# Two heads alternate in halves of TensorE, and the PSUM banks are shared out anew

## The chip, the cores and the metric

The kernel runs on one core of a Trainium2 chip. A core has the engines PE (TensorE, matrix products), DVE (VectorE), ACT (ScalarE), POOL (GpSimd) and SP (SyncE, which here issues most DMAs), each with an instruction order of its own that it works through without overtaking; semaphores tie the orders together. PSUM, the memory that PE writes to, has eight banks of 512 fp32 values on each of 128 partitions. The metric is the device time of one execution in microseconds, the median of several.

PE's array of 128 rows by 128 columns can be used as two halves: two of 64 rows (the operands lie on partitions 0 to 63 or 64 to 127) or two of 64 columns (the result lies on the one or the other 64 partitions). Views of the profile write the used part ahead of a product's shape: `128*128` is the full array, `64*128` one half of the rows, `128*64` one half of the columns.

## The reference

The reference is a model of two blocks on 256 tokens of 1024 channels. The first block has two layers, each a mixer and a mixture of 16 experts; the second has four mixers.

```python
# first block, layer 0: gated linear attention beside dense attention (latent and context)
# first block, layer 1: attention in a window, 16 heads on 2 of keys and values, with a context and a sink
s = einsum('bqhgd,bkhd->bhgqk', q, k) * Dh ** -0.5
p = softmax(concatenate([where(mask, s, -inf), sink]))[..., :-1]
o = einsum('bhgqk,bkhd->bqhgd', p, v)
# second block: h = h + rms_norm(mixer(rms_norm(h))) four times, all causal, with linear biases
# 1 nsa: compressed, selected and window attention of 16 heads on 4, gated
p_s = masked_softmax(q @ ksel - slopes * dist, dist >= 0);  o_s = p_s @ vsel      # the same for the window
# 2 diff: p = masked_softmax(...) of two maps;  a = p[0] - lam * p[1];  o = a @ v
# 3 dilated: three groups of keys, merged by their log-sum-exp
o = sum(softmax(stack(lses)) * stack(outs))
# 4 stick: a = exp(log_sigmoid(logits) + between), between = reversed sums of log_sigmoid(-logits)
```

Every mixer ends with a gate silu(z) or the like and an output projection.

## The kernel before, in words

The kernel keeps all tokens on the chip and streams the weights (285 MB) past them. Large products are made exact enough by splitting both operands into a high and a low part of type float32r: `gemm` (L239) issues three products for each 128 channels, L243, L244 and L245, usually 256 columns wide. Scores are split the same way: `scores` (L414) issues L416, L417 and L418 for one head, whose 64 channels lie on one half of the partitions, so these products use half of the rows. Values are multiplied as plain fp32, which the profile records as two matmuls each; two heads use one half of the columns each (L915 in nsa, L1094 in `attend`, L719 and L720 in stick).

A head's way in nsa, diff and dilated: scores into a bank of PSUM; DVE adds the bias and takes the maximum (L891 in nsa); ACT takes the exponential and its sum (L893); PE turns the weights, three transposes into one bank (`turn_causal`, L438); ACT copies the bank to SBUF (L440); PE multiplies by the values. `attend` does the same for the even and the odd layer with `turn` (L1131: transposes L1141, copies L1143). In stick, a head's sums over later keys take products of their own (L710 to L712) between two passes of ACT.

The eight banks carry tags, taken from one pool for the whole kernel: two `mm` for projections, three `s` for scores, two `t` for turned weights and small products, one `o` for outputs. A tile of a tag waits until the oldest tile of the tag has been read.

In odd, `queries(0)` projects the first queries into an `mm` bank, `norm_rope` (L1044: square L1049, a product with ones L1051, root L267 and L268, times L1054) normalises them, then come the keys in the same way, the values, and the four rounds of four heads each, every round with the next round's queries ahead of its scores. The weights of the experts that follow are issued by SP behind those of odd's output projection.

A scheduler orders the instructions of each engine when the kernel is built; the order stays as it is on the chip. It takes the instructions in program order where it can and fills with others where its plan has an engine wait. nsa has 8 rounds of two heads with two branches each: 16 branches of two heads. Beside them stand the products of the gate and of the queries. Stick has 8 pairs of heads, diff 8 heads of two maps, dilated 4 heads of three groups.

Of the kernel before, what the change touches and what calls it, by code (L numbers as in the profile page):

```python
# [10 lines left out]
F32 = mybir.dt.float32  # L11
# [3 lines left out]
AF = mybir.ActivationFunctionType  # L15
# [28 lines left out]
def constants():  # L44
    """Arrays that depend on shapes alone: groups of them side by side in [128, n] arrays."""
# [36 lines left out]
    # GLA: sums over tokens up to / from t, over the gate's 16; which token pairs a level holds  # L82
# [14 lines left out]
    # rotary tables by channel of a pair of heads  # L97
# [10 lines left out]
class K:  # L108
    def __init__(self, ctx, tc, A, groups):
# [5 lines left out]
        self.ps = ctx.enter_context(tc.tile_pool(name="ps", bufs=1, space=PSUM))  # L115
# [34 lines left out]
    def psum(self, tag, bufs):  # L150
        return self.ps.tile([128, 512], F32, name="ps_" + tag, tag=tag, bufs=bufs)

    def mm(self):
        return self.psum("mm", 2)

    def pss(self):
        return self.psum("s", 3)

    def pst(self):
        return self.psum("t", 2)  # L160

    def pso(self):
        return self.psum("o", 1)
# [25 lines left out]
    def wload(self, src, kt=KT, pool=None, eng=None):  # L189
        """src: DRAM [kt*128, n] -> raw tile view [128, kt, n]."""  # L190
# [14 lines left out]
    def wload_parts(self, src, kt):  # L205
        """The same in the room of a split weight's parts; gives a list of [128, n]."""
# [32 lines left out]
    def gemm(self, out, sh, sl, mh, ml, ks=range(KT)):  # L239
        """out[M, N] = sum_k stat[k]^T mov[k], both given as hi, lo lists of [128, .]."""  # L240
# [6 lines left out]
    def gemm_cm(self, out, w, m, x):  # L247
        """channel-major: out[128 channels, tokens]"""
# [4 lines left out]
    def gemm_tm(self, out, w, t, x, cols=slice(None)):  # L253
        """token-major: out[128 tokens, columns]"""
# [1986 lines left out]
```

## Time and profile before

| | us |
|---|---|
| median of 3 runs | 1591.15 (1583.63 to 1591.83) |
| profiled execution: its span | 1586.3 |
| median less the span | 4.85 |

The profiled execution's time beyond its span is not among the runs; the span is what all views divide up. Its stages, from the first to the last instruction of each by PE's timeline:

| stage | from, to (us) |
|---|---|
| even layer | 0 to 387 |
| its experts | 387 to 629 |
| odd layer | 629 to 738 attention, to 764 output projection |
| its experts (latent alone) | 764 to 921.5 |
| nsa | 921.5 to 985 keys, values and first scores; to 1089 the rounds; to 1129 output projection |
| diff | 1129 to 1280 |
| dilated | 1280 to 1417 |
| stick | 1417 to 1586.3, its pairs from 1455 to 1557 |

Matmuls overlap in their pipeline, so PE's busy time runs from the first start to the last end of a row of products without a gap; how long one product holds the array is read from the distance between starts. Some records of matmuls can be missing from a trace.

### The profile page before, as it was taken

The page shows a single profiled execution, that of the slowest core. Times are in us where ns is not written, and L with a number is a line of the kernel's source. Part 1 is how long each engine was busy: PE and PEld are TensorE (multiplying, and loading weights), DVE is VectorE, ACT ScalarE, POOL GpSimd, SP SyncE. Part 2 cuts the span into 40 slices and gives each one's busy share as a digit, 9 for nine tenths or more (in the row PEclk, how much of TensorE's full clock was granted, in tenths as well). Part 3 has the DMA queues.
Part 4 walks back from the last instruction along what each step waited for, and adds up shares of the span by engine and source line. Part 5 has one row for each costly group of instructions (what it writes and reads, how often), then busy time and mean ns, then how long its engine had stood idle before and what let it go on. Part 6 is the DMA issues. An engine that isn't in the chain of part 4 may idle for free.

```text
span 1586.3 us, 26615 instructions
## 1 busy us (share of the span) xinstructions
PE 1467.7 (93%) x10361; PEld 1173.3 (74%) x10361; DVE 977.2 (62%) x2043; ACT 810.3 (51%) x1644; POOL 321.5 (20%) x311
## 2 busy tenths in 40 slices
PE   5999987989599898999799999999999999989998
PEld 3766765666477676766566688777899889889888
DVE  4654669853577556875412376555777685867665
ACT  3454544543466554664211345565556654746664
POOL 2000124412211103111000031232321241422231
PEclk7999999999799998999899999999999999999999
DMA  8700248964799987214899946121454445345320
GB/s 266 233 27 1 94 159 280 309 226 147 220 327 332 354 271 264 87 58 140 287 315 368 337 141 217 55 81 54 138 162 132 133 148 172 122 143 168 106 82 27
DMA packets 243689, 284.71 MB, mean 179 GB/s; under 512 B 14546, under 2 KB 227554, under 8 KB 243556
## 3 DMA queue, kind: packets, MB, share of 16 engines
q1 hardware_dynamic: 236644, 259.85, 50.6%
q0 software_dynamic: 6912, 23.07, 4.4%
q8 instruction: 85, 1.39, 0.4%
q14 instruction: 48, 0.39, 0.1%
HBM read 275.56 MB, written 9.44 MB: 180 GB/s over the span
## 4 chain that ended last, share of the span: by engine, by line
PE 44%; DVE 4%; ACT 1%; DMA 1%; issue 0%; POOL 0%; another core or an unknown queue 0%; DVEq 0%; POOLq 0%
PE ps_mm L243 6%; PE ps_mm L244 6%; PE ps_mm L245 5%; PE ps_mm L1954 4%; PE ps_mm L332 3%; PE ps_mm L546 2%; PE ps_s L416 2%; PE ps_t L1994 2%; PE ps_o L915 1%; PE ps_t L438 1%; PE ps_s L417 1%; DVE wl L231 1%; PE ps_s L418 1%; DMA w<-exp_w_gate 1%; PE ps_t L1937 1%; PE ps_s L546 1%
## 5 line engine op out<-in xcount | busy, mean ns | idle before, releaser
L231 DVE TENSOR_TENSOR wl<-w,wh 128x1024 fp32r<-128x1024 f32 x257 | 321.4, 1257 | 155.4 <-ACT wh L230 151.9
L230 ACT CAST wh<-w 128x1024 fp32r<-128x1024 f32 x261 | 270.3, 1042 | 139.3 <-PE ps_mm L245 67.6
L243 PE MATMUL ps_mm<-uh,wl 128*128 128x256 f32 x720 | 210.4, 292 | 0.7 <-DVE v L561 0.6
L244 PE MATMUL ps_mm<-ul,wh 128*128 128x256 f32 x720 | 205.6, 286 | 0.0
L245 PE MATMUL ps_mm<-uh,wh 128*128 128x256 f32 x720 | 204.3, 284 | 0.0
L243 PEld LDWEIGHTS ps_mm<-uh,wl 128*128 128x128 f32 x720 | 135.6, 188 | 8.2 <-issue 1.8
L244 PEld LDWEIGHTS ps_mm<-ul,wh 128*128 128x128 f32 x720 | 135.7, 188 | 3.3 <-issue 1.2
L245 PEld LDWEIGHTS ps_mm<-uh,wh 128*128 128x128 f32 x720 | 135.7, 188 | 1.9 <-issue 0.7
L243 PE MATMUL ps_mm<-wh,xl 128*96 128x256 f32 x256 | 76.6, 299 | 3.0 <-DVE xl L409 3.0
L244 PE MATMUL ps_mm<-wl,xt 128*96 128x256 f32 x256 | 75.0, 293 | 0.0
L245 PE MATMUL ps_mm<-wh,xt 128*96 128x256 f32 x256 | 73.9, 289 | 0.0
L1010 PE MATMUL ps_mm<-w,cond 128*32 128x256 f32 x768 | 55.3, 405 | 17.5 <-DMA w<-mod_w 8.7
L2036 PE MATMUL ps_s<-w,ht 128*96 128x512 f32 x128 | 57.6, 593 | 0.0
L1954 PE MATMUL ps_mm<-w,xt 128*64 128x256 f32 x384 | 52.7, 383 | 0.1
L243 PE MATMUL ps_mm<-hh,wl 128*128 128x512 f32 (+2 forms) x136 | 47.9, 353 | 2.5 <-DVE qn L1054 2.5
L1010 PEld LDWEIGHTS ps_mm<-w,cond 128*32 128x32 f32 x768 | 22.0, 113 | 37.8 <-DVE mod L1017 11.4
L295 POOL TENSOR_TENSOR rawsq<-rawsq 128x256 f32<-128x256 f32 x16 | 13.9, 869 | 177.7 <-ACT rawsq L294 177.7
L244 PE MATMUL ps_mm<-hl,wh 128*128 128x512 f32 (+2 forms) x136 | 48.0, 354 | 0.9 <-DVE hl L1035 0.9
L243 PEld LDWEIGHTS ps_mm<-wh,xl 128*96 128x96 f32 x256 | 43.5, 170 | 7.2 <-DVE xl L409 4.0
L245 PE MATMUL ps_mm<-hh,wh 128*128 128x512 f32 (+2 forms) x136 | 46.8, 344 | 0.0
L332 PE MATMUL ps_mm<-ol,wh 128*128 128x256 f32 x144 | 42.4, 295 | 3.6 <-DVE ol L587 3.6
L332 PE MATMUL ps_mm<-oh,wl 128*128 128x256 f32 x144 | 41.9, 295 | 2.9 <-ACT oh L587 1.7
(659 smaller groups left out, 4082.4 us busy)
## 6 DMA issues: line engine op xcount, KB each, us to landing
w<-mod_w SPq DMA_DIRECT2D x48, 1024.0 KB, 7.5
w<-exp_w_up SPq DMA_DIRECT2D x28, 1024.0 KB, 11.2
w<-exp_w_gate SPq DMA_DIRECT2D x27, 1024.0 KB, 13.5
w<-exp_w_down SPq DMA_DIRECT2D x27, 1024.0 KB, 11.7
w<-b_w_in SPq DMA_DIRECT2D x16, 1024.0 KB, 5.5
w<-d_w_in SPq DMA_DIRECT2D x16, 1024.0 KB, 5.5
w<-a_w_in SPq DMA_DIRECT2D x14, 1024.0 KB, 8.1
w<-c_w_in SPq DMA_DIRECT2D x14, 1024.0 KB, 5.0
```

Source lines behind the costliest of these rows:

```text
L230: nc.scalar.copy(hv, raw[:, i:i + c])
L231: (nc.gpsimd if i and pool_too else nc.vector).tensor_sub(lv, raw[:, i:i + c], hv.bitcast(F32))
L243: nc.tensor.matmul(out, sl(k), mh(k), start=k == ks[0], stop=False)
L244: nc.tensor.matmul(out, sh(k), ml(k), start=False, stop=False)
L245: nc.tensor.matmul(out, sh(k), mh(k), start=False, stop=k == ks[-1])
L332: nc.tensor.matmul(p[:, 256 * m:256 * m + 256], w[a][k][:, 128 * m:128 * m + 128], b[:, k], start=k == 0 and m == 0 and j == 0, stop=k == ...
L416: nc.tensor.matmul(out, ql, kh, start=True, stop=False)
L546: nc.tensor.matmul(ps[i][:, 256 * t:256 * t + 256], x[a][:, k, ts], w[b][k], start=k == 0 and t == 0 and j == 0, stop=k == KT - 1 and t == ...
L1010: nc.tensor.matmul(p[j:j + 32, :256], self.cond[:, k], w[:, k], start=k < 4, stop=k >= 4)
L1954: nc.tensor.matmul(p[64 * a:64 * a + 64, 256 * j:256 * j + 256], xt[:, k, off + 64 * a:off + 64 * a + 64], w[j][a][k], start=k == 0, stop= ...
L1994: nc.tensor.matmul(p[64 * a:64 * a + 64, :], ht[:, f, 64 * a:64 * a + 64], w[a][f][:, cs], start=f == 0, stop=f == 1)
L2036: nc.tensor.matmul(p, ht[:, f], w[:, f, cs], start=f == 0, stop=f == 1)
```

## The change

Scores of two heads, one on each half of PE's rows, are now issued in turn, product by product, into the two banks of one tile (`pair`); values of two heads, one on each half of the columns, are issued in turn, and the first of them is made to wait for both heads' turned weights (`behind`). In diff, dilated and one branch of nsa the first 128 queries are multiplied with 128 keys instead of 256. Dilated takes two heads in one pass and merges each behind the three groups of both. The pool of banks is opened anew ahead of odd and ahead of its experts: four banks become two two-bank tiles `s2`, and one `mm` (in odd) or one `t` (from the experts on) is given up for that. Odd's output projection and the experts' sums use the two-bank tiles; other small tiles of the experts take `t` and `o` in turn. Comments were taken out too; lines of the changed kernel are some 20 to 40 further down.

```diff
+    def banks(self, **n):
+        self.pstack.close()
+        self.ps = self.pstack.enter_context(self.tc.tile_pool(name="ps", bufs=1, space=PSUM, reuse_waits="tile"))
+        self.nbanks = n
+        self.either = itertools.cycle((self.pst, self.pso))
...
+    def pair(self):
+        if "s2" not in self.nbanks:
+            return [self.psum("s"), self.psum("s")]
+        t = self.ps.tile([128, 2, 512], F32, name="ps_s", tag="s2", bufs=self.nbanks["s2"])
+        return [t[:, 0], t[:, 1]]
...
+    def behind(self, ins, *others):
+        for o in others:
+            self.tc.add_manual_dep(ins, o.name, mybir.DependencyInfo(mybir.DependencyClass.Sync, mybir.DependencyReason.DATA), reason="side by side")
...
-    def scores(self, out, qh, ql, kh, kl):
-        nc.tensor.matmul(out, ql, kh, start=True, stop=False)
-        nc.tensor.matmul(out, qh, kl, start=False, stop=False)
-        nc.tensor.matmul(out, qh, kh, start=False, stop=True)
+    def scores(self, outs, qs, ks):
+        for j, (a, b) in enumerate(((1, 0), (0, 1), (0, 0))):
+            for out, q, k in zip(outs, qs, ks):
+                self.nc.tensor.matmul(out, q[a], k[b], start=j == 0, stop=j == 2)
+    def scores_causal(self, q, k, mq, mk):
+        pvs = [p.rearrange("p (t n) -> p t n", t=2) for p in self.pair()]
+        rs = (slice(0, 64), slice(64, 128))
+        for t in range(2):
+            ts, n = slice(128 * t, 128 * t + 128), 128 * t + 128
+            self.scores([pv[:, t, :n] for pv in pvs], [[x[r, mq, ts] for x in q] for r in rs], [[x[r, mk, :n] for x in k] for r in rs])
+        return pvs
...
+    def spread(self, po, vs, ats):
+        first = None
+        for kt, (of, n) in enumerate(((0, 256), (256, 128))):
+            for half, (at, _) in enumerate(ats):
+                i = self.nc.tensor.matmul(po[64 * half:64 * half + 64, 256 - n:256], vs[half][kt], at[:, of:of + n],
+                                          start=kt == 0, stop=kt == 1).ins
+                first = first or i
+        self.behind(first, *(i for _, i in ats))
...
 # dilated
-            for hd in range(H):
+            for j in range(H // 2):
+                es, mxs, sms = ([wk.tile([128, G, n], F32, name=name, tag=name, bufs=3) for _ in range(2)]
+                                for name, n in (("e", 384), ("mx", 2), ("sm", 2)))
                 for g in range(G):
+                    pvs = self.scores_causal(q[:2], q[2:], 2 * g + j, 2 * g + j)
...
+                for i, (e, mx, sm) in enumerate(zip(es, mxs, sms)):
+                    self.merge(wk, e, mx, sm, v, 2 * j + i, o)
...
 # stick
-                        nc.tensor.matmul(po[r, :256], v[:, 0, vs], a[:, :256], start=True, stop=False)
-                        nc.tensor.matmul(po[r, 128:256], v[:, 1, vs], a[:, 256:384], start=False, stop=True)
+                    ps = self.pair()
+                    rs = (slice(0, 64), slice(64, 128))
+                    for ks, qs, os in ((slice(0, 128), slice(0, 256), slice(0, 256)), (slice(128, 256), slice(128, 256), slice(256, 384))):
+                        self.scores([p[:, os] for p in ps], [(kh[r, m, ks], kl[r, m, ks]) for r in rs],
+                                    [(qh[r, m, qs], ql[r, m, qs]) for r in rs])
+                    ats = [self.stick_weights(wk, p, suffix, before, minus, diag) for p in ps]
+                    self.spread(po, [[v[:, kt, 64 * (hd + i):64 * (hd + i) + 64] for kt in range(2)] for i in range(2)], ats)
...
 # odd's output projection; the experts of the latent
+            outs = self.pair() + self.pair()
-                p = self.mm()
+            for p, (c, w) in zip(outs, enumerate(ws)):
...
-                acc = [self.pss() for _ in range(3)] + [self.pso()]
+                acc = self.pair() + self.pair()
-                        p = self.pst()
+                        p = next(self.either)()
...
 # nsa, keys of the blocks
-                p = self.mm() if i else self.pss()
+                if i:
+                    p = self.mm()
+                else:
+                    p, ph = self.pair()
...
 # program
+            self.banks(mm=1, s2=2, t=2, o=1)
             self.odd(mods[1][:, 2])
+            self.banks(mm=2, s2=2, t=1, o=1)
             self.moe_lat(1, moe[1], self.x, gsf[1], mods[1][:, 3], mods[1][:, 5], ahead=(
```

The order of PE shows what moved. First a pair of heads in stick, before (L416 to L418 are scores, L243 and L244 the gate's products; 128x256 is the result):

```order
L243 MATMUL ps_mm_15328<-uh_14823,wl_15325 128x256
L416 MATMUL ps_s_15259<-qkh_15076,qkl_15142 128x256
L417 MATMUL ps_s_15259<-qkl_15077,qkh_15141 128x256
L418 MATMUL ps_s_15259<-qkh_15076,qkh_15141 128x256
L416 MATMUL ps_s_15259<-qkh_15076,qkl_15142 128x128
L417 MATMUL ps_s_15259<-qkl_15077,qkh_15141 128x128
L418 MATMUL ps_s_15259<-qkh_15076,qkh_15141 128x128
L416 MATMUL ps_s_15284<-qkh_15076,qkl_15142 128x256
L417 MATMUL ps_s_15284<-qkl_15077,qkh_15141 128x256
L418 MATMUL ps_s_15284<-qkh_15076,qkh_15141 128x256
L416 MATMUL ps_s_15284<-qkh_15076,qkl_15142 128x128
L417 MATMUL ps_s_15284<-qkl_15077,qkh_15141 128x128
L418 MATMUL ps_s_15284<-qkh_15076,qkh_15141 128x128
L244 MATMUL ps_mm_15328<-ul_14824,wh_15324 128x256
```

and after (L438 is the one line of all scores now, L263 the gate's; `x2` are the two heads, one bank each of tile ps_s_15161):

```order
L265 MATMUL ps_mm_15107<-uh_14778,wh_15103 128x256
L438 MATMUL ps_s_15161<-qkh_15030,qkl_15096 128x256 x2
L438 MATMUL ps_s_15161<-qkl_15031,qkh_15095 128x256 x2
L438 MATMUL ps_s_15161<-qkh_15030,qkh_15095 128x256 x2
L438 MATMUL ps_s_15161<-qkh_15030,qkl_15096 128x128 x2
L438 MATMUL ps_s_15161<-qkl_15031,qkh_15095 128x128 x2
L438 MATMUL ps_s_15161<-qkh_15030,qkh_15095 128x128 x2
L263 MATMUL ps_mm_15280<-uh_14778,wl_15273 128x256
```

The twelve products stay together; the heads take turns where one followed the other.

Second, two branches in nsa's rounds, before (L438 are the transposes, L915 the values):

```order
L438 MATMUL ps_t_10059<-k_all_68,e_10045 128x128 x3
L915 MATMUL ps_o_10020<-at_10043,vsw_9170 64x256
L416 MATMUL ps_s_10189<-KH_9275,ql_9953 128x256
L417 MATMUL ps_s_10189<-KL_9276,qh_9952 128x256
L438 MATMUL ps_t_10081<-k_all_68,e_10069 128x128 x3
L418 MATMUL ps_s_10189<-KH_9275,qh_9952 128x256
L416 MATMUL ps_s_10189<-KH_9275,ql_9953 128x256
L417 MATMUL ps_s_10189<-KL_9276,qh_9952 128x256
L418 MATMUL ps_s_10189<-KH_9275,qh_9952 128x256
L244 MATMUL ps_mm_10845<-ul_9145,wh_10836 128x256
L245 MATMUL ps_mm_10845<-uh_9144,wh_10836 128x256
L243 MATMUL ps_mm_10845<-uh_9144,wl_10841 128x256
```

and after, in the eighth to thirteenth branch (L467 are the transposes, L438 scores, L477 values):

```order
L467 MATMUL ps_t_10317<-k_all_68,e_10310 128x128 x3
L467 MATMUL ps_t_10330<-k_all_68,e_10323 128x128 x3
L438 MATMUL ps_s_10457<-KH_9263,ql_10225 128x128 x2
L438 MATMUL ps_s_10457<-KL_9264,qh_10224 128x128 x2
L438 MATMUL ps_s_10457<-KH_9263,qh_10224 128x128 x2
L438 MATMUL ps_s_10457<-KH_9263,ql_10225 128x256 x2
L438 MATMUL ps_s_10457<-KL_9264,qh_10224 128x256 x2
L438 MATMUL ps_s_10457<-KH_9263,qh_10224 128x256 x2
L477 MATMUL ps_o_10292<-at_10321,vsw_9158 64x256
L477 MATMUL ps_o_10292<-at_10334,vsw_9158 64x256
L477 MATMUL ps_o_10292<-at_10321,vsw_9158 64x128
L477 MATMUL ps_o_10292<-at_10334,vsw_9158 64x128
```

Transposes, scores and values come in blocks of two heads, and from the seventh branch's end to the thirteenth's no product of the gate or the queries stands between them; before, such products stand in every round.

Third, the start of odd, before (L245 ends the keys' product, L1051 are the ones-products of queries and keys, L243 begins the next):

```order
L244 MATMUL ps_mm_6409<-hl_6054,wh_6405 128x512
L245 MATMUL ps_mm_6409<-hh_6053,wh_6405 128x512
L1051 MATMUL ps_t_6384<-nsq_6382,k_rope_6301 128x512
L1051 MATMUL ps_t_6436<-nsq_6434,k_rope_6301 128x512
L243 MATMUL ps_mm_6455<-hh_6053,wl_6402 128x512
```

and after (L1086 is the ones-product, here of the keys; that of the queries stands 25 rows ahead of it, before the keys' first product):

```order
L264 MATMUL ps_mm_6413<-hl_6054,wh_6409 128x512
L265 MATMUL ps_mm_6413<-hh_6053,wh_6409 128x512
L1086 MATMUL ps_t_6440<-nsq_6438,k_rope_6305 128x512
L263 MATMUL ps_mm_6459<-hh_6053,wl_6406 128x512
L264 MATMUL ps_mm_6459<-hl_6054,wh_6405 128x512
```

Each ones-product now stands between two projections, where both stood behind both projections.

## Rows read from the trace of the kernel before

**Rows 1.** The page: busy us, share of the span and instructions of each engine.

```profile
PE 1467.7 (93%) x10361; PEld 1173.3 (74%) x10361; DVE 977.2 (62%) x2043; ACT 810.3 (51%) x1644; POOL 321.5 (20%) x311
```

**Rows 2.** Busy time by stretch: us, PE, PEld, DVE, ACT, POOL, clock, DMA share, GB/s.

```profile
629.00:738.00 109.00, 106.59 (x652) 74.86 (x652) 79.62 (x168) 66.22 (x137) 11.33 (x10) 1.00 0.22 70
...
764.00:921.50 157.50, 148.15 (x1075) 93.83 (x1073) 49.23 (x134) 38.30 (x81) 0.06 (x1) 0.97 0.94 317
...
985.00:1089.00 104.00, 103.78 (x709) 79.87 (x707) 57.32 (x223) 63.69 (x185) 32.37 (x31) 1.00 0.21 69
1089.00:1129.00 40.00, 33.65 (x241) 29.79 (x241) 22.61 (x39) 19.06 (x36) 6.04 (x6) 0.96 0.34 106
...
1455.00:1557.00 102.00, 101.81 (x752) 90.85 (x751) 64.36 (x91) 62.58 (x117) 29.87 (x35) 1.00 0.30 94
```

**Rows 3.** PE's timeline in stick: start, us, line, operation, tiles, used array, shape.

```profile
1454.77 0.28 PE L244 MATMUL ps_mm<-ul,wh 128*128 128x256 f32 x1
1454.89 0.27 PE L245 MATMUL ps_mm<-uh,wh 128*128 128x256 f32 x1
1455.09 0.38 PE L416 MATMUL ps_s<-qkh,qkl 64*128 64x256 f32 x1
1455.31 0.28 PE L417 MATMUL ps_s<-qkl,qkh 64*128 64x256 f32 x1
1455.43 0.28 PE L418 MATMUL ps_s<-qkh 64*128 64x256 f32 x1
...
1456.07 0.27 PE L418 MATMUL ps_s<-qkh 64*128 64x128 f32 x1
1456.27 0.39 PE L243 MATMUL ps_mm<-uh,wl 128*128 128x256 f32 x1
```

**Rows 4.** PE's timeline in odd: scores of two heads, then of one.

```profile
705.99 0.51 PE L416 MATMUL ps_s<-KH,ql 64*128 64x512 f32 x2
706.32 0.42 PE L417 MATMUL ps_s<-KL,qh 64*128 64x512 f32 x2
706.55 0.42 PE L418 MATMUL ps_s<-KH,qh 64*128 64x512 f32 x2
706.79 0.39 PE L416 MATMUL ps_s<-KH,ql 64*128 64x512 f32 x1
707.02 0.38 PE L417 MATMUL ps_s<-KL,qh 64*128 64x512 f32 x1
```

**Rows 5.** PE's timeline in nsa: values of two heads, then of one.

```profile
998.61 0.86 PE L915 MATMUL ps_o<-at,vsw 128*64 128x256 f32 x6
999.40 0.55 PE L438 MATMUL ps_t<-k_all,e 128*128 128x128 f32 x3
...
1012.30 0.65 PE L915 MATMUL ps_o<-at,vsw 128*64 128x256 f32 x2
1012.88 0.66 PE L926 MATMUL ps_t<-k_all,rb 128*128 128x128 f32 x4
```

**Rows 6.** ACT by line in nsa, 985 to 1089: count | busy, mean ns | idle before.

```profile
L893 ACT ACTIVATE e<-e,mx 128x256 f32<-128x256 f32 x29 | 14.6, 502 | 0.0
L440 ACT COPY at<-ps_t 128x384 f32<-128x384 f32 x27 | 12.8, 478 | 31.2 <-PE ps_t L438 31.0
L893 ACT ACTIVATE e<-e,mx 128x128 f32<-128x128 f32 x29 | 11.7, 404 | 2.6 <-DVE mx L891 2.5
L893 ACT ACTIVATION_READ_ACCUMULATOR e<-e,mx 128x1 f32 x58 | 11.2, 193 | 0.0
```

**Rows 7.** ACT and DVE by line in odd, 629 to 738: the norm of projections.

```profile
L267 ACT ACTIVATE nrs<-ps_t,eps 128x512 f32<-128x512 f32 x5 | 3.4, 683 | 1.4 <-DVE nsink L1491 0.9 <-PE ps_t L1051 0.5
...
L268 ACT ACTIVATE nrs<-nrs 128x512 f32<-128x512 f32 x5 | 3.2, 631 | 0.2
L1054 DVE SCALAR_TENSOR_TENSOR qn<-ps_mm,gq,nrs 128x512 f32<-128x512 f32 x4 | 3.0, 749 | 3.5 <-ACT nrs L268 3.4
...
L1049 ACT ACTIVATE nsq<-ps_mm 128x512 f32<-128x512 f32 x5 | 2.9, 583 | 2.8 <-PE ps_mm L245 2.8
```

More of the change, by code (lines that the diff above doesn't have):

```diff
@@ L114, in __init__ @@
         self.wraw = ctx.enter_context(tc.tile_pool(name="wraw", bufs=5))
-        self.ps = ctx.enter_context(tc.tile_pool(name="ps", bufs=1, space=PSUM))
+        self.pstack = ctx.enter_context(ExitStack())
+        self.banks(mm=2, s=3, t=2, o=1)
         nc.scalar.preload_act_table_set("natural_log_exp_and_others")
@@ L539, in values @@
         x, (last_a, last_b) = self.raw, self.raw_last
-        ps = [(self.mm if i < 2 else self.pss)() for i in range(len(parts))]
+        ps = [self.mm(), self.mm()] + (self.pair() if len(parts) > 2 else [])
         def product(i, w, k):
@@ L731, in stick, with stick_weights @@
             self.out_last(pool, rows, oh, ol, w_out, gain, out)
+    def stick_weights(self, wk, ps, suffix, before, minus, diag):
+        nc = self.nc
+        l = wk.tile([128, 384], F32, name="l", tag="l")
+        nc.scalar.copy(l, ps[:, :384])
+        sp = wk.tile([128, 512], F32, name="sp", tag="sp")
+        s3 = sp[:, :384]
+        nc.vector.scalar_tensor_tensor(s3, l, -1.0, l, op0=ALU.mult, op1=ALU.min)
+        nc.scalar.activation(s3, s3, AF.Exp)
+        nc.scalar.activation(s3, s3, AF.Ln, bias=1.0)
+        nc.vector.scalar_tensor_tensor(s3, l, 0.0, s3, op0=ALU.max, op1=ALU.add)
+        nc.gpsimd.tensor_mul(diag(sp), diag(sp), before)
+        pc = self.pst()
+        nc.tensor.matmul(pc[:, :256], suffix, sp[:, :256], start=True, stop=False)
+        nc.tensor.matmul(pc[:, 128:256], self.ones, sp[:, 256:384], start=False, stop=True)
+        nc.tensor.matmul(pc[:, 256:384], suffix, sp[:, 256:384], start=True, stop=True)
+        a = wk.tile([128, 512], F32, name="a", tag="a")
+        nc.vector.tensor_sub(a[:, :384], l, pc[:, :384])
+        nc.gpsimd.tensor_add(diag(a), diag(a), minus)
+        return a, nc.scalar.activation(a[:, :384], a[:, :384], AF.Exp).ins
     def nsa(self, h, gpre, gpost, ahead=None):
@@ L869, in nsa @@
                     for br in (1, 0):
+                        ps = self.pair()
+                        rs = (slice(0, 64), slice(64, 128))
+                        cols = ((0, 0, 128), (256, 0, 256)) if br == 0 else ((0, 16, 144), (144, 16, 272))
+                        ko = 16 + S if br == 0 else 0
+                        for t, (c0, skip, n) in enumerate(cols):
+                            ts = slice(128 * t, 128 * t + 128)
+                            self.scores([p[:, c0:c0 + n] for p in ps], [(qh[r, m, ts], ql[r, m, ts]) for r in rs],
+                                        [(KH[r, g, ko:ko + n], KL[r, g, ko:ko + n]) for r in rs])
                         ats = []
@@ L1090, in attend @@
             ats = [self.turn(wk, lambda t: e[:, t], kts) for e in es]
+            first = None
             for kt in range(kts):
-                for a, at in enumerate(ats):
-                    nc.tensor.matmul(po[64 * a:64 * a + 64, 256 * b:256 * b + 256], v(kt), at[:, kt], start=kt == 0, stop=kt == kts - 1)
+                for a, (at, _) in enumerate(ats):
+                    i = nc.tensor.matmul(po[64 * a:64 * a + 64, 256 * b:256 * b + 256], v(kt), at[:, kt], start=kt == 0, stop=kt == kts - 1).ins
+                    first = first or i
+            self.behind(first, *(i for _, last in ats for i in last))
         if sink is not None:
@@ L1134, in turn @@
         at = wk.tile([128, kts, S], F32, name="atk", tag="atk")
+        last = []
         for b in range(kts // 2):
@@ L1976, in moe_down @@
         nc = self.nc
-        pt = self.pst()
+        pt = next(self.either)()
         for f in range(2):
@@ L1990, in moe_down @@
             cs = slice(512 * j, 512 * j + 512)
-            p = self.pst()
+            p = next(self.either)()
             for f in range(2):
```

165 lines of the change are left out of this document (57 added, 108 removed).

## The prediction

> **What bounds the kernel now.** I read the page's first part: TensorE is busy for 93% of the span [rows 1]. An average over eight stages says little, so next came the busy time by stretch [rows 2]. There the reader is to see two kinds. In odd's attention (629 to 738 us) PE is busy 106.59 of 109 us, in nsa's 103.78 of 104, in stick's 101.81 of 102: these are bound by PE, and what PE is spared there can come back. The latent's experts (764 to 921.5) move 317 GB/s at a DMA share of 0.94: they are bound by their weights, and nothing on PE pays. In nsa VectorE and ScalarE are busy 57.32 and 63.69 of 104 us, in odd 79.62 and 66.22 of 109.
>
> Then I read PE's timeline from start to start, because its busy time counts overlapping work. In stick a full-array product starts 0.12 us after the one before it. The first 64-row product starts 0.20 us after the last full one, the second 0.22 us after the first, and only then is it 0.12 again; on the way back the first start is 0.20 away once more [rows 3]. A change between full array and halves so costs (0.20 − 0.12) + (0.22 − 0.12), about 0.19 us by the unrounded starts. That two halves work beside each other is already to be seen: in odd two 512-wide products start together and the next two 0.33 and 0.23 us later, while a lone one holds its half for 0.23 us all the same [rows 4]. With the columns split it is alike: four value products of two heads, alternated, stand 0.79 us ahead of the next transposes; one head's single 256-wide product stands 0.58 us [rows 5]. Less the 0.19 of the change, one head's 256 columns cost 0.39 and its 128 columns by proportion 0.20, four products one after the other 1.18, alternated 0.60: 0.58 us saved for a pair of heads.
>
> **The change part by part.** What PE is spared if nothing else is late next; counts are from the two instruction orders, and those of products that already run beside each other are from PE's starts in the trace (neighbours within 0.03 us).
>
> Odd: mode changes 78 to 34, 44 × 0.19 = 8.4 us. Of 96 scores of 512 columns 24 start beside their neighbour, after it 48 can: 24 × 0.23 = 5.5. Of 128 value records 47 run beside another, 64 can: 17 × 0.2 = 3.4. Together 17.3.
> Nsa: mode changes 155 to 78, 77 × 0.19 = 14.6. Of 192 score products 24 run beside another, 96 can: 72 × 0.12 = 8.6 (one in four of the 256-wide now has 128 columns, but in rows like these 144 columns still start 0.11 apart, so I give that nothing more). Values: 16 branches × 0.58 = 9.3, of which about a quarter is had already: 7. Together 30.
> Stick: mode changes 58 to 37, 21 × 0.19 = 4.0. Scores: 19 more of the 256-wide beside another, 19 × 0.12 = 2.3, the 128-wide 24 × 0.06 = 1.4. Values: before, each head's two stand alone, 8 × 0.58 = 4.6. Together 12.
> Dilated: 29 × 0.12 + 8 × 0.19 = 5. Diff: 25 × 0.12 = 3, less four more changes, 2. Even: 15 × 0.23, 3. The experts: 0, by their DMA share; their weights stand behind odd's on SP's queue, so I let them start earlier by what odd gains.
> The sum is 69 us: the upper end, with PE always fed. The comments taken out cost nothing.
>
> What is late next, stage by stage.
> Odd now has one bank for its projections instead of two. Before, the queries' and keys' products stand in a row with both norms behind them; now each product waits until the one before it is squared, averaged, its root taken and its bank read: 0.58 + 0.68 + 0.63 + 0.75 us [rows 7] plus the ones-product and the steps between engines, some 4 us, twice, before the first scores. Behind the waiting product stand all other products on PE. That is 8 of 17; VectorE, busy 79.62 of 109 before, would be at 80% of what is left. I take 7 back, bounds 0 and 14.
> Nsa has one bank for turned weights instead of two. Each head's turning waits for ScalarE's copy of the one before, 0.48 us [rows 6]; that is hidden as long as other products stand between. In the first seven of 16 branches 312 of the gate's and queries' products do: 312 × 0.12 + 7 × 3.1 (a branch's own PE work: 12 pairs of scores and turnings at 0.11 to 0.12, 0.6 of values, four changes) = 59 us. In the next six none stands, and ScalarE sets the pace: two heads' 0.50 + 0.40 + 2 × 0.19 + 0.48 = 1.77 each [rows 6], 3.5 a branch; with the chain not perfectly filled I take 4.4: 27 us. The last three stand between the output projection's 72 products and lengthen its 40 us by some 5. That is 59 + 27 + 45 = 131, against 104 + 40 = 144 us before [rows 2]; 2 more are saved in the 64 us ahead of it, where the first scores are. So 15, bounds 3 and 30.
> Stick: products of the gate and the queries stand between every step of a pair, 26 to 48 of them between the suffix sums of its two heads; the wait added (the first value product stands behind both heads' weights) has them as cover, 3 to 6 us. I take 10, bounds 5 and 12; if the cover is gone it is one head's exponential, 0.5 us, at each of 8 pairs.
> Dilated: both merges of the last pair now end late, on VectorE, ahead of the output projection: I take 3, bounds −4 and 5. Diff 2 (0 to 2), even 2 (0 to 3).
> The sum: 7 + 15 + 10 + 3 + 2 + 2 = 39. The profiled execution spans 1586.3 us; 39 less is 1547.3. The runs' median of 1591.15 lies 4.85 above the span, so the forecast is 1552 us. By the lower bounds it would be 4 us less than before, by the upper 66.
>
> **The rivals.**
> *All of it comes back.* The copies and exponentials keep up, and 66 to 69 us go: 1591 − 67 = 1524. For it: VectorE and ScalarE have idle time in every one of these stretches [rows 2]. Against it: six branches of nsa without any other product, and the single bank in odd.
> *The emptying of banks takes PE's place.* A branch of nsa takes 6.5 us before (104 / 16). If turning, copy, turning, copy and the exponentials of two heads follow each other on the one bank, a branch is 2 × (1.28 + 0.48) for ScalarE, 2 × 0.33 for the turnings, and VectorE's passes and the steps between engines, an estimate of 1 us a head: 6.2. Then nsa gains 5 in place of 15, odd's norms eat its gain, stick keeps 5, the others 2: 12 us, 1579. For it: the copy of turned weights already waits only on PE, 31 us in all [rows 6], so it is the next link. Against it: in seven branches other products lie between. The Trainium skill, "TensorEngine Tiling (Array Packing)", Performance Considerations, says that tiling makes TensorE faster but not the emptying of PSUM, whose copies may become the limit. By that rule the outcome is this rival's; the trace of before does not show it yet, with ScalarE at 63.69 of 104 us.
> *Slower: the order fixed beforehand makes PE wait at the single turning bank.* Each engine works through its order without overtaking. If the order puts the second head's turning where the first one's copy, or the second's exponential, is not done, PE stands with everything behind it. There are 44 turnings in nsa, diff and dilated and 16 suffix sums in stick, 60 places. A full miss, a head's exponentials and copy, is 1.8 us [rows 6]: 108 us against 69 gained, 1630. It decides from 77 / 60 = 1.3 us a place. For it: the bank for turning is halved, and PE waits nowhere today, 103.78 of 104 [rows 2]. Against it: only twelve of these turnings have no other product near them.
> *The halves do not run beside each other.* Then only the changes are spared, 146 × 0.19 = 28, less what odd and the single bank take back: 1585 to 1591. Rows 4 and 5 speak against it.
>
> **How the numbers follow.** The forecast with its own range, 1533 to 1570, has 0.58; all of it back 0.10; the emptying of banks 0.20; slower 0.09; no work side by side 0.03. About 0.5% (8 us) is what a measurement here can tell from no change. Of the third case 0.12 lies beyond 8 us and 0.08 within; so faster 0.58 + 0.10 + 0.12 = 0.80, same 0.11, slower 0.09. The range for eight in ten leaves out the slower case and the farther half of the first rival: 1522 to 1590, no more than the bounds of the parts (4 to 66 us) allow.
>
> **What would show it.** In the profile after: two 64-row products of one kind starting together in stick and nsa, and the twelve of a pair in stick over in about 0.9 us instead of 1.17; nsa's 13 us for two branches falling to about 9 where no other product stands, with PE idle there and released by the copy of turned weights; gaps on PE of some 4 us, twice, at odd's start, released by the norm; the experts' stretch as long as before but earlier; stick shorter by about 10 us. It would be wrong if the stretch in nsa without other products came out at 6 us a branch or more, if PE showed waits for the copy of turned weights in stick and diff as well, or if odd did not get shorter at all.

## The result and the profile after

The changed kernel takes 1606.85 us (median of 4 runs, 1606.68 to 1609.21), the kernel before in the same comparison 1588.74: a ratio of 1.0124, 95% interval 1.0098 to 1.0149. It is slower by 18 us, where 39 us less were forecast. The profiled execution took 1606.68 us, its span is 1605.0.

The page of the changed kernel, PE's busy time and the granted clock in 40 slices (compare [rows 1]):

```profile
PE 1437.2 (90%) x10361; PEld 1158.7 (72%) x10361; DVE 976.0 (61%) x2043; ACT 811.2 (51%) x1644; POOL 319.6 (20%) x311
...
PEclk7999999999799999899899999989999989989999
```

PE is busy 30 us less than before and the span is 19 us longer: what was spared came back as idle time, and more. The mean granted clock fell from 0.970 to 0.948. In the trace the clock is at one of two levels, 1.2 and 2.4 GHz; it is at the lower for 98 us of the kernel before and for 169 us of the changed one, and PE is busy in 65 and 122 us of that time.

Busy time by stretch (us, PE, PEld, DVE, ACT, POOL, clock, DMA share, GB/s), against [rows 2]:

```profile
629.80:658.00 28.20, 19.86 (x84) 14.75 (x83) 17.49 (x38) 12.42 (x24) 3.64 (x3) 0.85 0.40 132
658.00:741.00 83.00, 77.26 (x558) 56.89 (x558) 63.65 (x130) 54.67 (x115) 7.82 (x7) 0.99 0.17 56
741.00:796.00 55.00, 41.30 (x297) 30.15 (x294) 22.23 (x72) 16.48 (x33) 5.28 (x6) 0.88 0.90 303
...
997.00:1096.00 99.00, 86.96 (x688) 70.40 (x687) 55.23 (x210) 63.31 (x178) 34.78 (x31) 0.92 0.27 86
...
1434.00:1470.00 36.00, 27.31 (x189) 26.23 (x188) 26.80 (x44) 17.96 (x35) 11.09 (x12) 0.86 0.46 148
1470.00:1578.00 108.00, 108.00 (x912) 102.07 (x911) 75.65 (x102) 71.50 (x129) 34.59 (x35) 1.00 0.31 98
```

Before, PE was busy 106.59 of 109 us in odd; now it is 19.86 of 28.2 at odd's start and 77.26 of 83 behind it, the start at a clock of 0.85. In nsa's rounds it is 86.96 of 99, before 103.78 of 104. The 36 us ahead of stick's pairs have 27.31 at a clock of 0.86.

By stages, from PE's starts in the profiled executions (stage ends: the router's first product, odd's last values, the experts' first gathered product, their last sum, the last product of each closing norm, the end of the last result), in us more or less than before:

| run | median, ratio to before | even | experts, odd's attention | odd's output, routing | latent's experts | nsa | diff | dilated | stick |
|---|---|---|---|---|---|---|---|---|---|
| before (us) | 1588.74 | 386.8 | 351.8 | 46.3 | 136.0 | 205.4 | 150.5 | 137.0 | 169.6 |
| changed | 1606.85, 1.012 | −0.8 | +3.2 | +8.2 | −0.9 | −1.2 | +5.8 | +5.8 | −1.5 |
| seq | 1612.03, 1.017 | −1.1 | −1.5 | +7.0 | −0.5 | +6.0 | +7.6 | +7.4 | +0.8 |
| val | 1586.72, 1.001 | +0.1 | +3.4 | +8.2 | −0.2 | +1.6 | −3.2 | −2.5 | −5.0 |
| val_odd2 | 1600.27, 1.008 | −0.4 | +16.9 | +8.8 | +0.2 | +4.3 | −3.3 | −2.5 | −5.6 |
| val_t2 | 1713.66, 1.078 | +0.5 | +1.3 | +12.0 | −0.3 | +23.3 | +33.9 | +30.2 | +29.6 |
| val_outs | 1576.10, 0.992 | −0.8 | +4.7 | +1.6 | +0.3 | −3.7 | −3.2 | −2.5 | −5.0 |
| turn_mm | 1567.50, 0.989 | −0.3 | +2.0 | +1.6 | +0.6 | −10.2 | −4.6 | −3.7 | −6.0 |
| s4 | 1597.46, 1.007 | −0.5 | +2.2 | 0.0 | +0.1 | +16.6 | −4.1 | −0.1 | −5.6 |
| old_alt | 1570.22, 0.991 | −0.6 | +0.7 | +1.5 | −0.3 | −12.6 | +1.3 | +1.0 | −9.3 |
| old_nowait | 1579.83, 0.994 | +3.9 | −3.8 | +1.4 | −0.6 | −6.0 | 0.0 | +0.3 | −0.5 |
| old_seq | 1564.61, 0.985 | −0.1 | −2.7 | +1.8 | +1.1 | −14.9 | −0.2 | −0.3 | −8.0 |
| bef_vals | 1569.71, 0.988 | +0.3 | −2.8 | +1.8 | −0.5 | −9.3 | −0.2 | −0.1 | −7.3 |
| mix | 1562.05, 0.984 | −0.8 | −0.6 | +0.2 | +0.2 | −12.4 | −4.3 | −2.5 | −5.2 |

A stage is one execution's; most that an edit does not touch differ by 1 or 2 us from run to run. nsa differs by more: PE has one and the same order there in the changed kernel, val and val_outs, and nsa took 204.2, 207.0 and 201.7 us.

That the halves do run beside each other is plain. PE in stick, a pair of heads, against [rows 3]:

```profile
1486.10 0.28 PE L265 MATMUL ps_mm<-uh,wh 128*128 128x256 f32 x1
1486.31 0.39 PE L438 MATMUL ps_s<-qkh,qkl 64*128 64x256 f32 x2
1486.53 0.28 PE L438 MATMUL ps_s<-qkl,qkh 64*128 64x256 f32 x2
1486.65 0.28 PE L438 MATMUL ps_s<-qkh 64*128 64x256 f32 x2
1486.77 0.22 PE L438 MATMUL ps_s<-qkh,qkl 64*128 64x128 f32 x2
1486.83 0.28 PE L438 MATMUL ps_s<-qkl,qkh 64*128 64x128 f32 x2
1486.94 0.28 PE L438 MATMUL ps_s<-qkh 64*128 64x128 f32 x2
1487.15 0.39 PE L263 MATMUL ps_mm<-uh,wl 128*128 128x256 f32 x1
```

Each row is two heads' products that start together; the pair takes 0.84 us from its first start to the gate's next product, where it took 1.18.

What came in between shows ahead of stick's pairs. PE's timeline, and VectorE's below it:

```profile
1458.38 0.28 PE L580 MATMUL ps_s<-wh,rawh 128*128 128x256 f32 x1
1464.50 0.58 PE L263 MATMUL ps_mm<-uh,wl 128*128 128x256 f32 x1 [5.84 <-DVE v L595]
1464.88 0.41 PE L264 MATMUL ps_mm<-ul,wh 128*128 128x256 f32 x1
1465.09 0.41 PE L265 MATMUL ps_mm<-uh,wh 128*128 128x256 f32 x1
```

```profile
1460.23 1.67 DVE L251 TENSOR_TENSOR wl<-w,wh 128x1024 fp32r<-128x1024 f32 x1
1461.83 1.08 DVE L338 TENSOR_TENSOR ul<-u,uh 128x256 fp32r<-128x256 f32 x3
1462.84 1.21 DVE L251 TENSOR_TENSOR wl<-w,wh 128x1024 fp32r<-128x1024 f32 x1
1463.97 0.86 DVE L595 TENSOR_SCALAR v<-ps_mm,rcol 128x256 f32<-128x256 f32 x2
```

L580 are the value products, L263 is the first query product. It wants a projection bank that still holds values; VectorE reads that bank (L595) only behind two splits of weights (L251) and three steps of the input's low part (L338). PE stands for 5.84 us, and then its products start 0.21 us apart instead of 0.12. In the instruction order these 24 query products stand ahead of the fourth value product's 48, which have their bank and wait for nothing on VectorE but their weights; before, they stand behind all 48. The same happens in diff and dilated, with 22 and 21 query products. PE's waits for L595 there, all three mixers together (us in total, times, longest):

```profile
PE ps_mm L263 <- DVE v L595: 14.0, 3, 6.0
```

In odd, PE's waits at the start and behind it:

```profile
PE ps_mm L263 <- DVE qn L1089: 5.3, 4, 2.2
PE ps_t L1086 <- ACT nsq L1084: 3.4, 2, 2.8
PE ps_o L1131 <- DVE atk L1183: 1.5, 1, 1.5
```

They are the two norms that the one projection bank lets show: 8.7 us in the first two rows, where the kernel before has 1.3 us of such waits. In odd's output projection a wait is new that nobody forecast:

```profile
PE ps_s L263 <- DVE xT L1585: 1.7, 3, 0.6
...
PE ps_s L263 <- DVE wl L251: 0.8, 1, 0.8
```

L1585 is VectorE's reading of one 256-column part of a two-bank tile; the next product into that tile waits until the reading is done, 0.6 us three times.

nsa's rounds in three parts, the first seven branches, the six without other products, and the rest with the output projection; then PE's waits in all three:

```profile
997.00:1060.70 63.70, 59.55 (x498) 52.28 (x497) 37.70 (x126) 40.63 (x105) 18.90 (x16) 0.97 0.36 116
1060.70:1094.00 33.30, 25.41 (x181) 16.83 (x180) 16.59 (x85) 20.68 (x71) 15.27 (x14) 0.83 0.10 33
1094.00:1134.00 40.00, 34.60 (x260) 30.74 (x259) 22.33 (x49) 18.71 (x41) 6.07 (x5) 0.93 0.21 61
```

```profile
PE ps_t L467 <- ACT at L469: 5.4, 9, 0.6
PE ps_t L467 <- DVE o L974: 2.6, 3, 1.1
```

Where no query product stands between, PE is busy 25.41 of 33.3 us at a clock of 0.83, and what it waits for most often is ScalarE's copy of turned weights, 0.6 us each time.

### The profile page after: what moved, and what is told of

It is laid out like the page before. It is cut to its first block, busy times and chain, and to the rows that moved or that the text cites. A ratio compares the mean times of both kernels' runs of the same rounds, so it can differ in the third digit from the quotient of the medians.

```text
span 1605.0 us, 26596 instructions
## 1 busy us (share of the span) xinstructions
PE 1437.2 (90%) x10361; PEld 1158.7 (72%) x10361; DVE 976.0 (61%) x2043; ACT 811.2 (51%) x1644; POOL 319.6 (20%) x311
## 4 chain that ended last, share of the span: by engine, by line
PE 41%; DVE 5%; ACT 2%; DMA 1%; issue 1%; POOL 0%; another core or an unknown queue 0%; DVEq 0%; ACTq 0%
PE ps_mm L263 6%; PE ps_mm L264 5%; PE ps_mm L265 5%; PE ps_mm L352 3%; PE ps_mm L1994 3%; PE ps_mm L580 3%; PE ps_s L438 2%; DVE wl L251 2%; PE ps_o L477 1%; PE ps_t L467 1%; PE ps_s L580 1%; ACT wh L250 1%; DMA w<-a_w_in 1%; PE ps_o L2034 1%; PE ps_s L2039 1%
## 5 line engine op out<-in xcount | busy, mean ns | idle before, releaser
L251 DVE TENSOR_TENSOR wl<-w,wh 128x1024 fp32r<-128x1024 f32 x257 | 321.8, 1259 | 165.6 <-ACT wh L250 162.3
L263 PE MATMUL ps_mm<-uh,wl 128*128 128x256 f32 x720 | 213.1, 296 | 17.7 <-DVE v L595 14.0
L265 PE MATMUL ps_mm<-uh,wh 128*128 128x256 f32 x720 | 207.8, 289 | 0.0
L263 PEld LDWEIGHTS ps_mm<-uh,wl 128*128 128x128 f32 x720 | 139.7, 194 | 23.9 <-DVE v L595 14.5
L264 PEld LDWEIGHTS ps_mm<-ul,wh 128*128 128x128 f32 x720 | 139.7, 194 | 2.0 <-issue 1.1
L265 PEld LDWEIGHTS ps_mm<-uh,wh 128*128 128x128 f32 x720 | 139.5, 194 | 1.0 <-issue 0.7
L263 PE MATMUL ps_mm<-wh,xl 128*96 128x256 f32 x256 | 75.9, 296 | 2.4 <-DVE xl L429 2.4
L263 PE MATMUL ps_mm<-hh,wl 128*128 128x512 f32 (+2 forms) x136 | 49.6, 364 | 6.6 <-DVE qn L1089 6.6
L263 PEld LDWEIGHTS ps_mm<-wh,xl 128*96 128x96 f32 x256 | 42.8, 167 | 6.6 <-DVE xl L429 3.4
L1491 POOL TENSOR_TENSOR xk<-d,KD 128x512 f32<-128x512 f32 x27 | 39.0, 1454 | 29.4 <-ACT d L1481 10.6
```

The lines of the kernel that those rows point to most:

```text
L251: (nc.gpsimd if i and pool_too else nc.vector).tensor_sub(lv, raw[:, i:i + c], hv.bitcast(F32))
L263: nc.tensor.matmul(out, sl(k), mh(k), start=k == ks[0], stop=False)
L264: nc.tensor.matmul(out, sh(k), ml(k), start=False, stop=False)
L265: nc.tensor.matmul(out, sh(k), mh(k), start=False, stop=k == ks[-1])
L1491: nc.gpsimd.tensor_mul(xk, d, Ks)
```

## The experiments

**The order behind the values (val).** Each value product gets a tile of its own again:

```diff
-        ps = [self.mm(), self.mm()] + (self.pair() if len(parts) > 2 else [])
+        ps = [(self.mm if i < 2 else self.pss)() for i in range(len(parts))]
```

> The changed kernel with one edit: the third and fourth value products of diff, dilated and stick write the first banks of two two-bank tiles instead of the two banks of one. In the instruction order the fourth value product then stands ahead of the first query or key product again. Theory A (the early query products make TensorE wait 5.1, 6.0 and 5.8 us for the first value banks, with some us at half clock behind each): 1606.9 less 17 to 24, so 1583 to 1590, and no gap over 2 us behind the values. Theory B (the single bank for turned weights is what costs): 1603 to 1607.

Measured 1586.72 us: 20 us less than the changed kernel, the same as before (ratio 1.0006, 0.9982 to 1.003). PE's waits for L595 in the three mixers:

```profile
PE ps_mm L263 <- DVE v L595: 1.2, 2, 0.9
```

14.0 us became 1.2; diff, dilated and stick lost 9.0, 8.3 and 3.6 us, 21 together. Theory A holds, and theory B, with 1603 at least, is out.

**Two projection banks in odd (val_odd2).**

```diff
-            self.banks(mm=1, s2=2, t=2, o=1)
+            self.banks(mm=2, s2=2, t=1, o=1)
```

> As the run val, and odd too has two banks for projections and one for turned weights. Theory A with odd's norms as a second cost: the waits of 2.8, 2.2, 0.7 and 2.2 us at odd's start shrink to about 1, 6 to 9 us less than the run val. Rival (one bank for turning costs odd as much as one for projections): within 3 us of the run val, with gaps released by the copies of turned weights in odd.

1600.27 us: neither. Odd's norms no longer showed, but its attention got 13.5 us longer than in the run val, for the single turning bank. PE's waits in odd:

```profile
PE ps_t L1181 <- DVE atk L1183: 6.3, 7, 1.2
PE ps_t L1181 <- ACT atk L1183: 5.5, 8, 0.7
PE ps_o L1131 <- DVE atk L1183: 4.1, 5, 1.4
```

With two-bank tiles for scores, odd needs its two turning banks more than its two projection banks; the bank given up there was the cheaper one.

**Odd's output projection in separate tiles (val_outs).**

```diff
-            outs = self.pair() + self.pair()
+            outs = [self.mm(), self.pss(), self.pss(), self.pso()]
```

> The run val with odd's output projection in four tiles of a bank each (one for projections, the first banks of two two-bank tiles, the one for outputs) in place of two two-bank tiles. Theory (a product into one half of a tile waits for the reading of the other half, 0.58 us four times, and the clock falls behind it): the stretch from the last values of odd to the experts' first product, 54.6 us in the run val and 46.3 before, comes down to 47 to 49, the whole to 1578 to 1581. Rival (the weights arrive too late there): 53 to 55, 1585 to 1588.

1576.10 us: the stretch came down from 54.6 to 47.9 us, as forecast, and the waits for L1585 are gone. They were 1.7 us, with 0.8 for a split of weights (L251) that is gone too; no wait names the rest of the 6.7. The whole lies 2 us below its forecast: nsa, whose order the edit leaves alone, came out 5 us shorter too. So a tile of two banks is one thing to the order and its waits, though the products go to different banks. That holds for pools opened as these are, with `reuse_waits="tile"`; no run has another setting.

**Two turning banks from the experts on (val_t2).**

```diff
-            self.banks(mm=2, s2=2, t=1, o=1)
+            self.banks(mm=1, s2=2, t=2, o=1)
```

> The run val with the banks from the experts on shared as one for projections, two two-bank tiles, two for turning, one for outputs. Theory (nsa lost its gain to the one bank for turning): nsa, 207.0 us in the run val and 192.8 with the old banks, comes down to 190 to 196; the projections of all four mixers now wait for their one bank, so the whole may be anywhere from 1565 to 1610. Rival (the two-bank tiles themselves hold nsa back, since both heads' softmax must be done before a pair's tile is free): nsa stays over 202.

1713.66 us, far over the 1610 given as the most, and no answer on nsa: with one projection bank every mixer is 23 to 34 us slower. PE's waits behind the experts:

```profile
PE ps_mm L263 <- DVE sz L611: 9.9, 3, 3.5
PE ps_mm L263 <- DVE qkl L432: 9.6, 10, 1.4
...
PE ps_mm L263 <- DVE sz L558: 7.1, 3, 3.5
```

**Four single score banks (s4).** In odd and behind it:

```diff
-            self.banks(mm=1, s2=2, t=2, o=1)
+            self.banks(mm=1, s=4, t=2, o=1)
-            self.banks(mm=2, s2=2, t=1, o=1)
+            self.banks(mm=2, s=4, t=1, o=1)
```

> The changed kernel with four score banks of one bank each in place of two tiles of two; one bank for projections in odd, one for turning from the experts on, as changed. If it is the sharing of one tile by two banks that costs (the early query products behind the values, the waits of odd's output projection): 1570 to 1582, near the run val_outs. If the single banks for projections and turning cost all of it: 1600 to 1607. nsa stays at 200 to 207 in either case, since one bank for turning still draws the query products together (312 of them in the first seven branches in this order too).

1597.46 us. The waits of the shared tile are gone, odd's output is at 0.0 and diff at −4.1, but nsa, expected at 200 to 207, took 222.0, at a clock of 0.88: both theories missed. With separate tiles the order no longer keeps a pair's scores of nsa together (by PE's starts 3 of the 48 products of each shape start beside another, where 24 would be all pairs and the changed kernel has 22 to 24), and the one bank for turning is still there. Against val_outs, which has the tiles of two and the same bank for turning, nsa is 20 us longer: for the scores the shared tile was worth having.

**The second head of nsa turned elsewhere (turn_mm),** on top of val_outs:

```diff
-                            ats.append(self.turn_causal(wk, e))
+                            ats.append(self.turn_causal(wk, e, self.mm() if half else None))
```

> The run val_outs (1576.1, nsa 201.7), with the second head's turned weights of nsa in a bank for projections instead of the one for turning; the order of TensorE then spreads the query and gate products over all branches. Theory (one bank for turning, by the waits and by the order drawn up for it, takes nsa's gain): nsa 188 to 196, the whole 1562 to 1571. Rival (the alternated products leave too little work beside the softmax whatever the bank): nsa 199 to 205.

1567.50 us, nsa 195.2 instead of 201.7: both inside the theory's ranges, nsa outside the rival's. The step is only somewhat larger than nsa's spread from run to run, 201.7 to 207.0, and the intervals of the two ratios, 0.986 to 0.993 and 0.989 to 0.995, overlap; the run mix below has the same edit, and nsa took 193.0 there. The order now has query products in four groups between the branches, and PE's waits for ScalarE's copies of turned weights, 5.4 us in nine times in the changed kernel's nsa, are gone from the head of the list; what stands there is the softmax itself (L932 is the exponential):

```profile
PE ps_mm L467 <- ACT e L932: 3.0, 6, 0.6
PE ps_t L467 <- ACT e L932: 2.5, 6, 0.8
```

The edit changes both, the bank and the order that follows from it; the two weren't separated.

**The alternation with the old banks (old_alt).** No new banks; the output projection, the experts' sums and the values as before; the pair takes two of the three score banks.

```diff
-            self.banks(mm=1, s2=2, t=2, o=1)
-            self.banks(mm=2, s2=2, t=1, o=1)
-            outs = self.pair() + self.pair()
+                p = self.mm()
...
-                acc = self.pair() + self.pair()
+                acc = [self.pss() for _ in range(3)] + [self.pso()]
```

> The alternation of scores and values alone, out of the banks of the kernel before (two for projections, three single score banks, two for turning, one for outputs); odd's output projection and the experts as before. If the new shares of the banks cost and the alternation pays, this lies under the kernel before: 1550 to 1575. Rival (a pair takes two of three score banks, so the next pair's scores wait for the softmax of both): 1585 or more.

1570.22 us, ratio 0.991 (0.988 to 0.994): the change without the banks' new shares is worth 16 us, and with them it is 37 slower. nsa is 12.6 us faster, against 1.2 with the new banks. That gain is not the scores': with the old banks the order parts most pairs, and in nsa 12 score products start beside another, of 96 that could, as good as before (13), against 92 in the changed kernel.

**Scores head after head, with the new banks (seq) and the old (old_seq).** The same edit in both:

```diff
-        for j, (a, b) in enumerate(((1, 0), (0, 1), (0, 0))):
-            for out, q, k in zip(outs, qs, ks):
+        for out, q, k in zip(outs, qs, ks):
+            for j, (a, b) in enumerate(((1, 0), (0, 1), (0, 0))):
```

> The changed kernel with the scores of a pair head after head instead of in turn; banks, waits and values as in the changed kernel. If alternation is worth what the starts say (about half of the scores' time in odd, nsa, stick and the others, some 20 us), 1620 to 1635. Rival (TensorE is not what these stages wait for any more): 1603 to 1611.

> The run old_alt with the scores head after head; values, waits and the shorter causal scores stay. If the scores' alternation is what brings the 16 us against the kernel before: 1582 to 1590. Rival (values side by side, and fewer mode changes by blocks of two heads, bring most): 1571 to 1577.

seq 1612.03 us, 5 more than the changed kernel, short of the 13 expected at least and 1 over the rival's range; old_seq 1564.61, under every forecast and 6 less than in turn. The intervals of the ratios overlap in both comparisons, so neither difference is clear of noise. With the old banks few scores run beside each other in either run, so old_seq says little on the turns. With the new banks the order keeps the pairs together, and there the turns are not what pays. Why shows in the run seq, where three products of one head stand ahead of three of the other in stick:

```profile
1491.10 0.39 PE L438 MATMUL ps_s<-qkh,qkl 64*128 64x256 f32 x2
1491.32 0.28 PE L438 MATMUL ps_s<-qkl,qkh 64*128 64x256 f32 x2
1491.44 0.29 PE L438 MATMUL ps_s<-qkh 64*128 64x256 f32 x2
```

The rows are two products each all the same: the first of the second head starts 10 ns after the first of the first head, though three places behind it. The pair takes 0.84 us here too.

**Without the wait of the values (old_nowait).**

```diff
-        for o in others:
+        for o in ():
```

> The alternation out of the old banks (run old_alt, 1570.2) without the wait of the first value product for both heads' weights. If the wait is what keeps the values of two heads together on TensorE: mode changes come back, 5 to 12 us slower, 1575 to 1582. Rival (the wait only delays): 1565 to 1569.

1579.83 us against 1570.22, and a ratio to the kernel before of 0.9943 against 0.9908: the wait is worth 10 us by the medians and 6 by the ratios, each of which is to the kernel before in the same comparison. Without it 2 of nsa's 64 value records of 256 columns start beside another, with it 32, which is all pairs; in stick 0 and 16, and stick's 9.3 us are gone.

**The values alone, in the kernel before (bef_vals).** Two heads' values in turn and the first behind both heads' turned weights; nothing else of the change.

```diff
-                        nc.tensor.matmul(po[r, :256], v[:, 0, vs], a[:, :256], start=True, stop=False)
-                        nc.tensor.matmul(po[r, 128:256], v[:, 1, vs], a[:, 256:384], start=False, stop=True)
+                    self.spread(po, [[v[:, kt, 64 * (hd + i):64 * (hd + i) + 64] for kt in range(2)] for i in range(2)], ats)
```

> The kernel before with one part of the change alone: values of two heads in turn, the first behind both heads' turned weights; banks, scores and dilated as before. If the values bring most of what the alternation with the old banks brought (run old_seq, 1564.6, ratio 0.985): 1564 to 1572. If the scores in blocks of two heads and the shorter causal scores bring it: 1577 to 1588.

1569.71 us, ratio 0.988 (0.985 to 0.992): 18 of old_seq's 25 us, from one part of the change. In nsa and `attend` the values stood in turn already, so there the part is the wait alone.

**The parts that paid, together (mix).**

```diff
-            self.banks(mm=1, s2=2, t=2, o=1)
-            outs = [self.mm(), self.pss(), self.pss(), self.pso()]
+        for (j, (a, b)), (out, q, k) in ([(t, h) for t in terms for h in heads] if "s2" in self.nbanks else [(t, h) for h in heads for t in terms]):
```

> The parts that paid, together: odd with the banks of the kernel before, its output projection in them, scores there head after head (as in the run old_seq, where odd gained 2.7 us); from the experts on the two-bank tiles with scores in turn, separate tiles for the values, and the second head of nsa turned in a bank for projections (as in the run turn_mm: nsa less 10.2, diff 4.6, dilated 3.7, stick 6.0 against before). If the stages add up: 24 to 27 us under the kernel before, ratio 0.983 to 0.985. If the stages behind odd only got their gain at the price of odd's banks, or the change of banks at the experts costs a wait of its own: ratio 0.988 or more.

1562.05 us, ratio 0.984 (0.982 to 0.987): faster than both kernels, and by as much as the stages promised. Old_seq's interval, 0.981 to 0.988, overlaps it; which of the two is better stays open.

## Why the prediction was wrong

- *The spared PE time* was sized well, but not at the clock that came. Mode changes fell as counted (nsa 155 to 78, stick 58 to 37), nearly all pairs of scores and values run side by side, and a pair of stick takes 0.84 us (0.9 forecast). With PE's busy time at the lower clock counted half, an estimate, it fell by 59 us of the 69 forecast. Of these 28 were lost again to the lower clock, and PE's idle time grew by 49 us (118.6 to 167.8): together 19 us more. What failed is the part on what is late next, which gave back 30 of the 69, and there first that it has no wait at the start of diff, dilated and stick: "Diff 2 (0 to 2)", "I take 3", "I take 10".
- *Diff, dilated, stick*: forecast −15, measured +10.1. The step looked at banks for turning and scores and left out the value products at each mixer's start, whose order behind the shared tile put some 24 waiting query products ahead of 48 ready ones. That is 21 us by the run val, after which these stages stand at −10.7: near the forecast, with stick half of its 10. The order showed it beforehand, in rows that the prediction did not look at.
- *Odd*: forecast −7, measured +3.2 and +8.2. The two norms were sized rightly (8 us, 8.7 by the waits). Yet in the attention, with the experts ahead of it, PE's idle time grew by 14 us instead of 10, and the lower clock took 3, against 14 us spared at full clock of 17 forecast (the same estimate). The output projection was taken as free: the shared tile cost 6.7 us there by val_outs.
- *Nsa*: forecast −15, measured −1.2. The bunching was read rightly from the order, but its six bare branches took 33.3 us instead of 27, some 5.5 each (the rival said 6.2), and the first seven 63.7 rather than 59, at clocks of 0.83 and 0.97; the rest took 40.0 instead of 45. (A branch's own PE work is given as 3.1 us, where its terms add up to 2.8.) By the same estimate PE was spared 24 us of 30; 14 came back as idle time and 9 by the clock, which the sum did not have. The rival of emptied banks was nearer here. The Trainium skill, "TensorEngine Tiling (Array Packing)", Performance Considerations, says that the copies out of PSUM may become the limit once tiling has sped TensorE up; it says so of a fourfold speed-up. The trace agrees for this stage in part, with 5.4 us in nine waits for copies of turned weights; elsewhere it was the order, not the copies.
- *The rival for slower* named the right mechanism, an order fixed beforehand in which PE waits with everything behind it, and the wrong place: it stood at the values, 14.0 us in three waits, not at the turnings.
- *The clock* was left out. The sum took every spared or lost microsecond at full clock; in the stretches with new gaps the granted clock is 0.83 to 0.88, so the work behind a gap takes longer too.
- *The range*, 1522 to 1590, is said to stay within the parts' bounds of 4 to 66 us, but these give 1525 to 1587.

Not settled: with the value products, odd's output and nsa's second bank put right (turn_mm) the kernel is 20 us faster than before, and with odd's old banks besides (mix) 24, not 39. In mix odd's attention gains 0.6 us where 7 were forecast, and stick 5.2 where 10 were; why is open.

## What to carry to other kernels

When banks or buffers are shared out anew, look in the new order for every place where an instruction that waits now stands ahead of ready ones, at the starts of stages too, and not only where the work was changed. A tile of two banks is one thing for waits: give each accumulation its own tile, unless the order has to be kept from parting two products, as with a pair's scores in nsa. Before restructuring for side-by-side work, put two heads' value products in turn and hold the first behind both heads' weights: that brought 18 us here with no bank moved, where the best runs have some 24.

## What the runs showed of the hardware

Products on two halves of TensorE need not start in the order in which they stand. In the run seq, and already in [rows 4] (there too the order has three products of one head ahead of three of the other), the first products of both heads start 10 ns apart: the second head's stands behind three of the first and starts ahead of two of them. In stick before, six products of one head stand ahead of six of the other. There the second head's first starts beside the first head's third:

```profile
1455.43 0.28 PE L418 MATMUL ps_s<-qkh 64*128 64x256 f32 x1
1455.44 0.38 PE L416 MATMUL ps_s<-qkh,qkl 64*128 64x256 f32 x2
```

Of the two products in the second row the first is the second head's; the other is the first head's fourth, which stands ahead of it in the order and starts at 1455.55. So the opening's "without overtaking" does not hold, by these starts, between products of two halves of PE. How far ahead a product is taken no run here shows: with six ahead only 5 of the 48 products of 256 columns in stick start beside another, where 24 would be all pairs. Products of two halves need to stand close, then, and not in turn.

The same gap of 2.47 us ahead of stick, with the same products behind it, left the clock alone in one kernel and halved it in the other. Before, then changed:

```profile
1411.00:1414.00 3.00, 3.00 (x22) 2.58 (x20) 2.11 (x3) 1.60 (x4) 0.00 (x0) 1.00 0.81 248
1414.00:1417.00 3.00, 0.53 (x3) 0.30 (x2) 1.64 (x4) 1.53 (x4) 0.62 (x1) 1.00 0.29 102
1417.00:1421.00 4.00, 3.58 (x27) 3.12 (x26) 3.97 (x8) 1.54 (x3) 1.36 (x3) 1.00 0.01 2
```

```profile
1431.00:1434.00 3.00, 3.00 (x23) 2.80 (x22) 2.10 (x3) 1.60 (x4) 0.10 (x1) 1.00 0.77 227
1434.00:1437.00 3.00, 0.53 (x3) 0.23 (x2) 1.43 (x4) 1.74 (x4) 0.40 (x1) 1.00 0.35 123
1437.00:1441.00 4.00, 3.62 (x18) 3.41 (x18) 3.96 (x7) 1.54 (x3) 1.36 (x3) 0.60 0.00 0
```

Ahead of the gap PE was busy 3.00 of 3 us in both at a clock of 1.00. Behind it the products start 0.12 us apart before and 0.21 in the changed kernel, for some 3 us, at the lower of the two levels, 1.2 GHz. What decides it no run here shows.
